# Two units of a gate projection computed with seven block products for eight, in a decoder trunk that TensorE bounds

## The chip, the core and the metric

The kernel runs on one core of a Trainium2 chip. The metric is the device time of one execution in microseconds (us). Of the kernel before there are three runs: 814.84, 815.72 and 815.72, median 815.72 us. Its profiled execution took 816.18 us, of which the profile's span covers 813.3 us; the remaining 2.9 us lie around the span. The engines are called by the profile's names: PE (TensorE), PEld (its weight loads), DVE (VectorE), ACT (ScalarE), POOL (GpSimd) and SP (SyncE, which issues most DMAs).

## The reference

One layer over 256 tokens with model width 2048, all in float32:

```
h = rmsnorm(x);  u = h @ W_in            # conv branch, recurrent branch, two merge gates ga, gb
ya, yb = short conv branch, gated linear recurrence branch
m = sigmoid(ga) * (ya @ W_A) + sigmoid(gb) * (yb @ W_B)
x = x + m @ W_o
gate = sigmoid(rmsnorm(x) @ W_pg)        # "the last gate", 2048 x 2048
x = x + gate * (p @ W_pp)
out = rmsnorm(x)
```

## The kernel before, in words

**Work items.** Every projection is cut into column groups of 512 output columns. A column group is cut into items: one item `c` holds 256 input features, that is two blocks of 128 features by 512 columns, stored side by side in 1024 columns. The program walks a list of items (`items`) in order; `pos` is the place in it. For an item PE multiplies two feature blocks by two token halves (128 tokens each): four block products. A block product is made of three matmuls (`triple`, L1057 to L1061), because each float32 operand is split into a high and a low part: high by high, high by low, low by high. So an item has 12 matmuls of 512 columns. They accumulate in PSUM banks, one bank for each pair of column group and token half.

**Weights.** SP loads weights into tiles called `raw` (128x2048 float32, 1 MB, two items of one column group; pool `wp`, three buffers, L136 and L155). `split` cuts one item: `cut` (L181 to L184) lets ACT copy the block rounded to float32r (`whi`, L182) and lets DVE subtract that from the block (`wlo`, L183). The pair `whi`, `wlo` has four buffers in `wp`; in the last gate six more lie in the pool `late`.

**Lead.** In the loop over `pos`, items up to `pos + ahead(pos)` are split before the matmuls of `pos` are traced. `ahead` (L1053) is three items, and in the last gate it grows by one for every four items, to eight. Loads run four items further. Before the last gate the four buffers hold the lead to three items: a split waits until PE has finished the item before the one it is at.

**Order.** The program is traced in Python; a scheduler then decides each engine's order from the traced order, the dependencies and its own estimates. `step` lets the epilogues (generators, one step for each item) queue behind the last split. `pinned` (L1106) forces ACT and DVE to keep the traced order for the instructions of one loop step; before, it is in force only from the end of the first `ga` group to shortly after the merged products were parked, not in the last gate.

**The stages at the end.** The output projection `W_o` has four column groups O0 to O3 (8 items each). When one is done, `ep_o` adds it to `x` on DVE (L840), squares it and spreads it on ACT (L841, L847), writes it to DRAM in four DMAs and reads it back (`turned`, L317 and L328, both on SP), transposes 32x32 blocks on DVE (L321), and after a lag of three items scales and splits the four feature blocks into the operand `x1T` (`put`, ACT L286 and DVE L287). The last gate, `W_pg`, has four column groups PG0 to PG3 whose stationary operand is `x1T`; item `c` of each needs feature blocks `2c` and `2c+1`. PG0 and PG1 are done one after the other, 8 items each; after each, `ep_pg` takes the sigmoid (ACT L881), multiplies by the parked `p @ W_pp` (DVE L884), adds to `x` (DVE L885), squares (ACT L886) and multiplies by the final gain on POOL (L893). PG3 is walked three times for its halves, and `ep_last`, `last_half` and `last_norm` end the program.

**Seven for eight, as it exists before.** For column groups 1 to 3 of the two merge gates the kernel already treats a column group of `ga` and the same of `gb` as a pair. Over one item place `c` (a "unit") a pair is a 2x2 by 2x2 block product: eight block products. Five of eight units, `SEVEN`, use Winograd's form with seven: four sums of weight blocks and four sums of token blocks are made first (`combine_weights`, L198, helped by adding DMAs; `token_sums`, L748), and the results are combined afterwards (`ep_products`, L719; `ep_gates`, L730). Units with seven are items of kind `S` (7 products, 21 matmuls), units with eight are two items of kind `C` (4 products each).

Of the kernel before, what the change touches and what calls it, by code (L numbers as in the profile page):

```python
# [15 lines left out]
P = 128  # L16
# [7 lines left out]
CW = 512  # L24
# [7 lines left out]
SEVEN = [()] + 3 * [(0, 2, 3, 5, 6)]  # L32
TOGETHER = [(0, 1), (1, 2), (3, 2)]
NARROW, Q = len(LEVELS), 32

# [12 lines left out]
def hybrid_kernel(ctx, tc, xT, x, pT, prm, gfin, masks, w_in, w_a, w_b, w_o, w_pg, w_pp, out):  # L48
# [58 lines left out]
    for gi, (kind, j, w, g, op) in enumerate(groups):  # L107
        if kind == "gb" and SEVEN[j]:
            continue
        for c in range(w.shape[2]):  # L110
            it = {"gi": gi, "kind": kind, "j": j, "c": c, "last": c == w.shape[2] - 1}
            if kind != "ga" or not SEVEN[j]:
                key = ("PP", j // 2) if kind == "PP" else (gi, c // 2)
                items.append(dict(it, w=(w, g, c), raw=key, slot=(j if kind == "PP" else c) % 2))
            elif c in SEVEN[j]:
                items.append(dict(it, kind="S", w=(w, g, c), raw=(gi, c)))
# [10 lines left out]
    def raw_of(pos):  # L127
        it = items[pos]
        if it["raw"] not in loaded:
            if it["kind"] == "S":  # L130
                t = tuple(
                    pools["st"].tile([P, n, CW], F32, tag=tag, bufs=bufs, name=nm(tag))
                    for tag, n, bufs in (("sA", 2, 2), ("sB", 1, 3))
                )
            else:
                t = wp.tile([P, 2, 2 * CW], F32, tag="raw", bufs=3, name=nm("raw"))  # L136
            loaded[it["raw"]] = t
        return loaded[it["raw"]]

    def load(pos):  # L140
        it = items[pos]
        if it["raw"] not in loaded:
            raw, (w, g, c) = raw_of(pos), it["w"]
            if it["kind"] == "S":
                for n, to in enumerate(raw):
                    nc.sync.dma_start(out=to.rearrange("p n x -> p (n x)"), in_=w[g + n, :, c, n * CW :])
            elif it["kind"] == "C":
                for n in range(2):
# [8 lines left out]
    def add_by_dma(behind=None):  # L157
        pos = next((n for n, it in enumerate(items) if it["kind"] == "S" and n not in pair_sums), None)
        if pos is not None:
# [18 lines left out]
    def pair_of(pool, n, tags=("whi", "wlo"), width=2 * CW):  # L178
        return tuple(pool.tile([P, width], F32R, tag=tag, bufs=n, name=nm(tag)) for tag in tags)

    def cut(hi, lo, src):  # L181
        a = nc.scalar.activation(out=hi, in_=src, func=AF.Copy)  # L182
        v = nc.vector.tensor_tensor(out=lo, in0=src, in1=hi.bitcast(F32), op=ALU.subtract)  # L183
        state["splits"] = (a.ins, v.ins)  # L184

    def split(pos, halves=(0, 1)):
        it = items[pos]
        load(pos)
        src = raw_of(pos)
        src = src[0].rearrange("p n x -> p (n x)") if it["kind"] == "S" else src[:, it["slot"], :]  # L190
        if pos not in parts:
            spare = pos >= gate and (pos - gate) % 10 >= 4
            parts[pos] = pair_of(pools["late"], 6) if spare else pair_of(wp, 4)
# [18 lines left out]
    last_group = len(items) - w_pg.shape[2]  # L212
    gate = len(items) - 4 * w_pg.shape[2]
    parked = next(n for n, it in enumerate(items) if it["kind"] == "A" and it["j"] == 3)
# [500 lines left out]

    def quarters(j):
        return [state[n][:, t * CW : (t + 1) * CW] for n in ("ga", "gb") for t in range(NT)]

    def ep_products(j, bk):  # L719
        for n in ("ga", "gb"):  # L720
            state[n] = t4(n, 1)
        a0, a1, b0, b1 = quarters(j)
        nc.scalar.activation(out=a0, in_=bk["P1"], func=AF.Copy)
# [4 lines left out]

    def ep_gates(j, n, bk):
        q = quarters(j)  # L730
        for t in range(NT):
            add(q[2 * n + t], q[2 * n + t], bk["c", n, t])
        for t in range(NT):
            d = q[2 * n + t]
# [10 lines left out]
    def ep_gb(j, psum):  # L745
        return ep_gate(j, "gb", psum)

    def token_sums():  # L748
# [5 lines left out]
        for first, n in TOGETHER:  # L754
# [12 lines left out]
            a11, a12, a21, a22 = Fv[:, :, 0, 0], Fv[:, :, 1, 0], Fv[:, :, 0, 1], Fv[:, :, 1, 1]  # L767
            s1, s2, s3, s4 = (Sv[:, :, i] for i in range(4))
            for out, u, v, op in (
                (s1, a21, a22, ALU.subtract), (s2, s1, a11, ALU.subtract),  # L770
                (s3, a11, a21, ALU.subtract), (s4, a12, s2, ALU.add),
            ):
                nc.vector.tensor_tensor(out=out, in0=u, in1=v, op=op)
            sums_of = tuple(v[:, first : first + n] for v in state["S"])
            fourth = tuple(v[:, 2 * c : 2 * (c + n) : 2, P:] for v in state["hT"])
            for (hi, lo), src in ((sums_of, Sv[:, :, :3]), (fourth, Sv[:, :, 3])):
                nc.scalar.activation(out=hi, in_=src, func=AF.Copy)
# [57 lines left out]
    def ep_o(j, psum):  # L835
# [10 lines left out]
        for t in range(NT):  # L846
            nc.scalar.activation(  # L847
                out=spread(x1, t), in_=blocks(xs[:, t, j * CW : (j + 1) * CW]), func=AF.Copy
            )
        x1 = yield from turned(x1, 3)  # L850
        for c in range(4):
            put(state["x1T"], j * 4 + c, x1[:, c * T : (c + 1) * T], gain(PRM_GPLE, j * 4 + c))
        if j == 3:
            tot = sc(2, "tot2", 1)
# [3 lines left out]
            )  # L858
            state["rstd2"] = rsqrt_of(tot, NT, D, "r2")

    def ep_pp(j, psum):
# [13 lines left out]
    def ep_pg(j, psum):  # L875
        xs, pw, gt = state["x"], state["pw", j], t4()
        junk = t4()
        for t in range(NT):
            s = slice(t * CW, (t + 1) * CW)
            d = xs[:, t, j * CW : (j + 1) * CW]  # L880
            nc.scalar.activation(  # L881
                out=gt[:, s], in_=psum[t], func=AF.Sigmoid, scale=state["rstd2"][:, t : t + 1]
            )
            nc.vector.tensor_tensor(out=gt[:, s], in0=gt[:, s], in1=pw[:, s], op=ALU.mult)  # L884
            nc.vector.tensor_tensor(out=d, in0=d, in1=gt[:, s], op=ALU.add)  # L885
            nc.scalar.activation(  # L886
                out=junk[:, s], in_=d, func=AF.Square,
                scale=D**-0.5, accum_out=state["ss3"][:, t * 6 + j : t * 6 + j + 1],
            )
        yield  # L890
        for t in range(NT):
            d = xs[:, t, j * CW : (j + 1) * CW]
            nc.gpsimd.tensor_tensor(out=d, in0=d, in1=state["gfin"][:, j * CW : (j + 1) * CW], op=ALU.mult)  # L893
# [159 lines left out]
    def ahead(pos):  # L1053

        return LEAD + min(max(pos - gate, 0) // 4, 5)

# [10 lines left out]

    def count_products(j):
        order = [it for it in items if it["kind"] in ("S", "C") and it["j"] == j]
        used.clear()  # L1070
# [15 lines left out]
    def unit_products(pos):  # L1086
        it = items[pos]
        c, h = it["c"], state["hT"]

# [10 lines left out]
        b22, t1, t3, t2, t4_ = sums.pop(pos)  # L1100
        s1, s2, s3 = (tuple(v[:, SEVEN[1].index(c), i] for v in state["S"]) for i in range(3))
        s4 = x_of(0, 1)
        for name, op, part in zip(names, (s4, x_of(0, 0), x_of(1, 0), s1, s3, s2, x_of(1, 1)),
# [15 lines left out]

    active = []  # L1120
    banks = {}
    psums = {}
    done = 0
    for pos, it in enumerate(items[:last_group]):
        mark = len(nc.cur_bb.bb.instructions)
        kind, j, c, last = (it[n] for n in ("kind", "j", "c", "last"))
        _, _, w, g, opname = groups[it["gi"]]
        nch = w.shape[2]
        if pos == gate:
            close_pool("back")  # L1130
            close_pool("m")
            open_pool("late", "left")
        if pos == parked:
# [4 lines left out]
            active.append(unpark())  # L1138
        if pos + 2 < len(items) and items[pos + 2]["kind"] == "S":
# [22 lines left out]
        if pos >= gate and c == 0:  # L1162
            load_pw(j)
        if pos == FIRST + 4:
# [13 lines left out]
        if kind in ("S", "C"):  # L1178
            if c == 0 and it.get("n", 0) == 0:
                count_products(j)  # L1180
                for name, tag in zip(("P6", ("c", 0, 1), "P5", "P7", "P1", ("c", 0, 0), ("c", 1, 0), ("c", 1, 1)), "ggggssss"):
# [36 lines left out]
        if last and kind not in ("S", "C"):  # L1218
# [110 lines left out]
```

## Time and profile before

| what | value |
|---|---|
| median of three runs | 815.72 us |
| profiled execution, its span | 816.18 us, 813.3 us |
| last gate begins on PE | 716.67 us into the span |
| last matmul begins | 804.23 us into the span |
| PE, DVE, ACT, POOL busy in the span | 803.0, 589.0, 458.3, 49.4 us |
| granted PE clock, mean of the span | 0.996 |

Times in the views count from the start of the span. A busy time counts each instruction from its start to its end; matmuls overlap, so the distance between the starts of two of them, and not their duration, is what one of them costs PE. In a timeline row the first number is the start, the second the time to the end of the last instruction of the row, `x4` the number of instructions merged in the row, and the bracket the idle time of the engine before it with what ended it.

### The profile page before, as it was taken

To read this page: it belongs to the slowest core of one execution; us is meant where nothing else is said; L and a number is where in the kernel's file an instruction comes from. 1 tells how busy PE (TensorE), PEld (TensorE's weight loads), DVE (VectorE), ACT (ScalarE), POOL (GpSimd) and SP (SyncE) were. 2 spreads that over 40 slices of the span, in tenths; PEclk is the share of its full clock that TensorE was granted. 3 is DMA by queue.
4 is the path that set the end of the run, shared out by engine and by line. 5 is a ranking of instruction groups with operands and counts; after the bars stand their busy time and mean duration, and the time that the engine had idled before them with its cause. 6 is when DMAs were issued, how large, how long until landed. Compare 5 with 4: busy or idle time off the path is not lost.

```text
span 813.3 us, 10660 instructions
## 1 busy us (share of the span) xinstructions
PE 803.0 (99%) x4059; PEld 664.8 (82%) x4059; DVE 589.0 (72%) x748; ACT 458.3 (56%) x617; POOL 49.4 (6%) x58
## 2 busy tenths in 40 slices
PE   9999999999999999999999999999999999999995
PEld 6888888888888888888888888888888888888885
DVE  6746588767776498767679988987988665677932
ACT  7576476465555466466456456456544456566623
POOL 1000000001000000000021210210000000000310
PEclk9999999999999999999999999999999999999998
DMA  9988565648867555647799996995844779887812
GB/s 337 389 309 290 196 206 168 235 134 274 253 236 255 184 184 201 207 157 262 269 328 295 317 312 209 318 313 203 255 160 173 277 255 323 302 268 255 309 43 103
DMA packets 52659, 198.52 MB, mean 244 GB/s; under 512 B 6784, under 2 KB 16256, under 8 KB 37888
## 3 DMA queue, kind: packets, MB, share of 16 engines
q1 hardware_dynamic: 43200, 174.78, 61.2%
q0 software_dynamic: 6384, 16.25, 8.4%
q10 hardware_dynamic: 3024, 6.82, 2.5%
q8 instruction: 31, 0.51, 0.2%
q14 instruction: 20, 0.16, 0.1%
HBM read 184.19 MB, written 13.63 MB: 243 GB/s over the span
## 4 chain that ended last, share of the span: by engine, by line
PE 96%; issue 1%; DMA 1%; ACT 0%; DVE 0%; POOLq 0%; POOL 0%
PE g L1059 29%; PE g L1061 29%; PE g L1060 29%; PE s L1060 3%; PE s L1061 3%; PE s L1059 3%; DMA raw<-in_w_pp 1%; PE s L497 1%; PE s L598 0%; PE s L617 0%; PE s L616 0%; PE s L615 0%; ACT xs L922 0%; DVE wlo L183 0%; PE s L589 0%
## 5 line engine op out<-in xcount | busy, mean ns | idle before, releaser
L183 DVE TENSOR_TENSOR wlo<-raw,whi 128x1024 fp32r<-128x1024 f32 (+1 forms) x264 | 319.8, 1227 | 160.9 <-ACT whi L182 159.0
L182 ACT ACTIVATE whi<-raw 128x1024 fp32r<-128x1024 f32 (+1 forms) x264 | 272.2, 1049 | 207.4 <-PE g L1061 172.6
L1059 PE MATMUL g<-whi,xh 128*128 128x512 f32 (+1 forms) x738 | 284.0, 385 | 0.0
L1060 PE MATMUL g<-wlo,xh 128*128 128x512 f32 (+1 forms) x738 | 283.9, 385 | 0.0
L1061 PE MATMUL g<-whi,xl 128*128 128x512 f32 (+1 forms) x738 | 283.7, 385 | 0.0
L1061 PEld LDWEIGHTS g<-whi,xl 128*128 128x128 f32 x738 | 138.7, 188 | 27.6
L1059 PEld LDWEIGHTS g<-whi,xh 128*128 128x128 f32 x738 | 138.7, 188 | 27.4
L1060 PEld LDWEIGHTS g<-wlo,xh 128*128 128x128 f32 x738 | 138.7, 188 | 27.3
L1060 PE MATMUL g<-wlo,mh 128*128 128x512 f32 x128 | 49.8, 389 | 0.0
L1061 PE MATMUL g<-whi,ml 128*128 128x512 f32 x128 | 49.8, 390 | 0.0
L1059 PE MATMUL g<-whi,mh 128*128 128x512 f32 x128 | 49.7, 389 | 0.0
L182 ACT ACTIVATE thi<-sA 128x1024 fp32r<-128x1024 f32 x15 | 15.9, 1062 | 32.6 <-DVE sA L714 20.3
L1060 PE MATMUL s<-wlo,xh 128*128 128x512 f32 x84 | 32.7, 389 | 0.0
L1059 PE MATMUL s<-whi,xh 128*128 128x512 f32 x84 | 32.7, 389 | 0.0
L1061 PE MATMUL s<-whi,xl 128*128 128x512 f32 x84 | 32.7, 389 | 0.0
L1061 PEld LDWEIGHTS g<-whi,ml 128*128 128x128 f32 x128 | 23.9, 188 | 5.2 <-DVE ml L791 0.3
L1059 PEld LDWEIGHTS g<-whi,mh 128*128 128x128 f32 x128 | 24.0, 188 | 5.0
L1060 PEld LDWEIGHTS g<-wlo,mh 128*128 128x128 f32 x128 | 24.0, 188 | 5.0
L1060 PE MATMUL g<-wlo,ybTh 128*128 128x512 f32 x64 | 24.9, 390 | 0.0
L1061 PE MATMUL g<-whi,ybTl 128*128 128x512 f32 x64 | 24.9, 390 | 0.0
L1060 PE MATMUL g<-wlo,yaTh 128*128 128x512 f32 x64 | 24.9, 389 | 0.0
L1061 PE MATMUL g<-whi,yaTl 128*128 128x512 f32 x64 | 24.9, 389 | 0.0
(218 smaller groups left out, 906.5 us busy)
## 6 DMA issues: line engine op xcount, KB each, us to landing
raw<-in_w_in SPq DMA_DIRECT2D x66, 1024.0 KB, 5.1
raw<-in_w_o SPq DMA_DIRECT2D x16, 1024.0 KB, 6.1
raw<-in_w_pg SPq DMA_DIRECT2D x16, 1024.0 KB, 6.6
sT<-in_w_in POOLq DMA_DIRECT2D x30, 512.0 KB, 9.6
raw<-in_w_in SPq DMA_DIRECT2D x28, 512.0 KB, 5.8
raw<-in_w_a SPq DMA_DIRECT2D x8, 1024.0 KB, 8.8
raw<-in_w_b SPq DMA_DIRECT2D x8, 1024.0 KB, 8.6
sA<-in_w_in SPq DMA_DIRECT2D x15, 512.0 KB, 7.7
```

The lines of the kernel that those rows point to most:

```text
L182: a = nc.scalar.activation(out=hi, in_=src, func=AF.Copy)
L183: v = nc.vector.tensor_tensor(out=lo, in0=src, in1=hi.bitcast(F32), op=ALU.subtract)
L497: nc.tensor.matmul(out, X[:, 0, h, s], X[:, 1, h, t], start=True, stop=True, tile_position=(0, i * n))
L1059: nc.tensor.matmul(psum, oh, hi, start=first, stop=False)
L1060: nc.tensor.matmul(psum, oh, lo, start=False, stop=False)
L1061: nc.tensor.matmul(psum, ol, hi, start=False, stop=last)
```

## The change

PG0 and PG1 become one pair. Its units `c` = 3 and 5 (`LATE_SEVEN`) are done with seven products, the other six with eight, so the last gate's list has 30 items instead of 32, in the order C C, C C, C C, S(3), C C, S(5), C C, C C, then PG2 and PG3 as before. Every load of the pair brings 512 KB of each column group instead of 1 MB of one. The weight sums are not helped by DMAs: `combine_late` makes them in place in `raw`. For one unit the work is spread over three loop steps: `split` cuts the first column group's block; the next step does two additions, the cut of one block of 512 columns, and two additions; the step after cuts the two blocks of 1024 columns that the sums now fill. `late_sums` makes the token sums for a unit within `ep_o` of O1 (unit 3) and O2 (unit 5). The lag in `ep_o` of O3 becomes seven. `whi`, `wlo` now have four buffers in `wp` and five in `late` and are handed out by `free_pair`; `late` also gets a fourth `raw` buffer. `ahead` grows by at most one until the second S item, and `pinned` is in force from the start of the last gate to that item. `ep_pg` of the first two groups takes four steps instead of two.

```diff
+LATE_SEVEN = (3, 5)
...
-        if kind == "gb" and SEVEN[j]:
+        if kind == "gb" and SEVEN[j] or (kind, j) == ("PG", 1):
             continue
+        units = {"ga": SEVEN[j % len(SEVEN)], "PG": LATE_SEVEN if j == 0 else ()}.get(kind, ())
...
+                n = it["c"] if it["j"] == 0 else 4 + 4 * (it["j"] - 1) + it["c"] // 2
+                spare = it["op"] == "x1T" and n and n % 4 == 0
+                pool, bufs = (pools["late"], 1) if spare else (wp, 3)
+                t = pool.tile([P, 2, 2 * CW], F32, tag="raw", bufs=bufs, name=nm("raw"))
...
+    rings = {"wp": 4 * [-1], "late": 5 * [-1]}
+
+    def free_pair(until):
+        names = [n for n in rings if n == "wp" or n in pools]
+        name = min(names, key=lambda n: rings[n][0])
+        rings[name] = rings[name][1:] + [until if until < last_group else len(items)]
+        return pair_of(pools.get(name, wp), len(rings[name]))
...
+    def combine_late(pos):
+        R = raw_of(pos)
+        (b11, b21), (b12, b22) = ([R[:, n, i * CW : (i + 1) * CW] for i in range(2)] for n in range(2))
+        add(b11, b11, b12)
+        add(b12, b12, b22)
+        ts = [pair_of(pools["late"], 1, ("bhi", "blo"), CW)]
+        cut(*ts[0], b22)
+        add(b22, b11, b22)
+        add(b21, b22, b21)
+        yield
+        for n in range(2):
+            hi, lo = free_pair(pos)
+            cut(hi, lo, R[:, n, :])
+            ts += [(hi[:, i * CW : (i + 1) * CW], lo[:, i * CW : (i + 1) * CW]) for i in range(2)]
+        b22, t1, t4_, t3, t2 = ts
+        sums[pos] = (b22, t1, t3, t2, t4_)
...
-        x1 = yield from turned(x1, 3)
+        x1 = yield from turned(x1, 3 if j < 3 else 7)
         for c in range(4):
             put(state["x1T"], j * 4 + c, x1[:, c * T : (c + 1) * T], gain(PRM_GPLE, j * 4 + c))
+        for c in LATE_SEVEN:
+            if c // 2 == j:
+                yield
+                yield from late_sums(c)
...
+    def late_sums(c):
...
+        add(F.rearrange("p r b t -> p r (b t)"), hi.bitcast(F32), lo.bitcast(F32))
+        yield
+        sums_of(F[:, 0, 0], F[:, 1, 0], F[:, 0, 1], F[:, 1, 1], [Sv[:, i] for i in range(4)])
+        yield
+        cut(*(v[:, LATE_SEVEN.index(c)] for v in state["late sums"]), Sv)
+        yield
...
-        return LEAD + min(max(pos - gate, 0) // 4, 5)
+        return LEAD + min(max(pos - gate, 0) // 4, 5 if pos > settled else 1)
...
+        for q in range(pos + 1, done):
+            if items[q]["kind"] == "S" and items[q]["op"] != "hT" and q not in sums:
+                next(combining.setdefault(q, combine_late(q)), None)
...
-            if kind == "C" and c == nch - 1 and it["n"] == 0:
-                ep_products(j, banks)
+            if pos == settled + 2 or it["op"] == "hT" and kind == "C" and c == nch - 1 and it["n"] == 0:
+                ep_products(it["op"], banks)
             unit_products(pos)
             if kind == "C" and c == nch - 1:
-                ep_gates(j, it["n"], banks)
+                ep_gates(it["op"], it["n"], banks)
...
-        if begun < pos < parked + 8:
+        if begun < pos < parked + 8 or gate <= pos <= settled:
             pinned(mark)
```

More of the change, by code (lines that the diff above doesn't have):

```diff
@@ L157, in add_by_dma @@
     def add_by_dma(behind=None):
-        pos = next((n for n, it in enumerate(items) if it["kind"] == "S" and n not in pair_sums), None)
+        pos = next((n for n, it in enumerate(items) if it["kind"] == "S" and it["op"] == "hT" and n not in pair_sums), None)
         if pos is not None:
@@ L212, in hybrid_kernel @@
     last_group = len(items) - w_pg.shape[2]
-    gate = len(items) - 4 * w_pg.shape[2]
+    gate = next(n for n, it in enumerate(items) if it["op"] == "x1T")
+    settled = max(n for n, it in enumerate(items) if it["kind"] == "S")
     parked = next(n for n, it in enumerate(items) if it["kind"] == "A" and it["j"] == 3)
@@ L746, in ep_gb, with sums_of @@
         return ep_gate(j, "gb", psum)
+    def sums_of(a11, a12, a21, a22, to):
+        s1, s2, s3, s4 = to
+        for out, u, v, op in (
+            (s1, a21, a22, ALU.subtract), (s2, s1, a11, ALU.subtract),
+            (s3, a11, a21, ALU.subtract), (s4, a12, s2, ALU.add),
+        ):
+            nc.vector.tensor_tensor(out=out, in0=u, in1=v, op=op)
     def token_sums():
@@ L767, in token_sums @@
             a11, a12, a21, a22 = Fv[:, :, 0, 0], Fv[:, :, 1, 0], Fv[:, :, 0, 1], Fv[:, :, 1, 1]
[L768 to L774, printed above, removed]
+            sums_of(a11, a12, a21, a22, [Sv[:, :, i] for i in range(4)])
+            three = tuple(v[:, first : first + n] for v in state["S"])
             fourth = tuple(v[:, 2 * c : 2 * (c + n) : 2, P:] for v in state["hT"])
-            for (hi, lo), src in ((sums_of, Sv[:, :, :3]), (fourth, Sv[:, :, 3])):
+            for (hi, lo), src in ((three, Sv[:, :, :3]), (fourth, Sv[:, :, 3])):
                 nc.scalar.activation(out=hi, in_=src, func=AF.Copy)
@@ L1066, in hybrid_kernel, with count_products @@
     used, left = {}, {}
-    def count_products(j):
-        order = [it for it in items if it["kind"] in ("S", "C") and it["j"] == j]
+    def count_products(gi):
+        order = [it for it in items if it["kind"] in ("S", "C") and it["gi"] == gi]
         used.clear()
@@ L1100, in unit_products @@
         b22, t1, t3, t2, t4_ = sums.pop(pos)
-        s1, s2, s3 = (tuple(v[:, SEVEN[1].index(c), i] for v in state["S"]) for i in range(3))
-        s4 = x_of(0, 1)
+        if it["op"] == "hT":
+            s1, s2, s3 = (tuple(v[:, SEVEN[1].index(c), i] for v in state["S"]) for i in range(3))
+            s4 = x_of(0, 1)
+        else:
+            s1, s2, s3, s4 = (tuple(v[:, LATE_SEVEN.index(c), i] for v in state["late sums"]) for i in range(4))
         for name, op, part in zip(names, (s4, x_of(0, 0), x_of(1, 0), s1, s3, s2, x_of(1, 1)),
@@ L1128, in hybrid_kernel @@
         nch = w.shape[2]
+        if kind == "O" and j == 2 and c == 0:
+            close_pool("back")
         if pos == gate:
-            close_pool("back")
             close_pool("m")
```

79 lines of the change are left out of this document (50 added, 29 removed).

## The prediction

> **What bounds the kernel now.** I read the page's busy shares and its chain first, then the table of stretches over the last gate, then PE's timeline.
>
> ```profile
> PE 803.0 (99%) x4059; PEld 664.8 (82%) x4059; DVE 589.0 (72%) x748; ACT 458.3 (56%) x617; POOL 49.4 (6%) x58
> ...
> PE 96%; issue 1%; DMA 1%; ACT 0%; DVE 0%; POOLq 0%; POOL 0%
> ```
> ```profile
> core 0: us, PE busy (x) PEld busy (x) DVE busy (x) ACT busy (x) POOL busy (x), PEclk, DMA share, GB/s
> 700.00:720.00 20.00, 20.00 (x90) 16.57 (x89) 11.12 (x14) 10.70 (x17) 0.00 (x0) 1.00 0.88 302
> 720.00:740.00 20.00, 20.00 (x90) 16.56 (x89) 14.76 (x18) 13.26 (x21) 0.72 (x1) 1.00 0.85 290
> 740.00:760.00 20.00, 20.00 (x90) 16.55 (x89) 15.21 (x14) 11.27 (x16) 4.06 (x2) 1.00 0.71 247
> 760.00:780.00 20.00, 20.00 (x90) 16.57 (x89) 15.61 (x14) 11.47 (x15) 4.29 (x2) 1.00 0.64 228
> 780.00:800.00 20.00, 20.00 (x118) 17.78 (x117) 6.02 (x13) 6.27 (x15) 3.08 (x3) 1.00 0.12 43
> ```
> ```profile
> 716.67 0.39 PE L1059 MATMUL g<-whi,xh 128*128 128x512 f32 x1
> 716.90 0.39 PE L1060 MATMUL g<-wlo,xh 128*128 128x512 f32 x1
> ...
> 792.83 0.28 PE L1059 MATMUL g<-whi,xh 128*128 128x256 f32 x1
> ```
>
> PE makes up 96% of the chain that ended last, and in the last gate it is never idle: 20.00 of 20 us in every stretch, at a granted clock of 1.00. So a matmul that goes is time that goes, and any wait of PE that comes is time that comes. What a matmul costs is the distance of starts. From 716.67 to the first 256-column matmul at 792.83 there are 24 items of 12 and 48 of the last group's first pass, 336 matmuls: 76.16 / 336 = 0.2267 us each. An item of 12 lasts 2.72 us, a unit with seven products (21 matmuls) 4.76.
>
> DVE has 4 to 9 us of each 20 left up to 780. That is little slack for a change that swaps PE work for DVE work in one short stretch, so the prediction is mostly a count of DVE's queue there.
>
> **The change, part by part.** *Removed:* one product for each of two units, 2 x 3 matmuls x 0.2267 = **1.36 us** of PE. Nothing else leaves the chain; this is the most that can be won, 0.17% of the time. What a measurement of this kernel can tell from no change is about 0.2%, 1.63 us, so even the full gain lies inside that.
>
> The Trainium skill, "TensorE: Matmul & The Clock Gate", section "Back-to-back issue gap", gives about 131 ns for each 512-column matmul in a sustained stream of weight loads and matmuls. By that the six would be worth an estimated 0.79 us; the trace's distance of starts differs (0.2267 us), and it decides.
>
> *Added on DVE and ACT.* The prices:
>
> ```profile
> L714 DVE TENSOR_TENSOR sA<-sA x15: 691/691/693, 439.6 to 593.2; 128x512 f32<-128x512 f32 x15
> ...
> L183 DVE TENSOR_TENSOR blo<-sB,bhi x15: 681/683/685, 441.4 to 595.0; 128x512 fp32r<-128x512 f32 x15
> ```
> ```profile
> 413.50 0.28 DVE L773 TENSOR_TENSOR tlo<-thi 128x128 f32<-128x128 f32 x1
> ...
> 414.23 0.28 DVE L773 TENSOR_TENSOR tlo<-thi,tlo 128x128 f32<-128x128 f32 x1
> ```
> ```profile
> 715.25 1.23 DVE L183 TENSOR_TENSOR wlo<-raw,whi 128x1024 fp32r<-128x1024 f32 x1 [1.49 <-ACT whi L182]
> 716.39 1.24 DVE L321 STREAM_TRANSPOSE t<-t 128x1024 f32<-128x1024 f32 x1
> 717.55 1.25 DVE L840 TENSOR_TENSOR xs<-xs,g 128x512 f32<-128x512 f32 x2
> 718.72 1.65 DVE L287 SCALAR_TENSOR_TENSOR xl<-t,prm_t,xh 128x256 fp32r<-128x256 f32 x4
> 720.29 1.22 DVE L183 TENSOR_TENSOR wlo<-raw,whi 128x1024 fp32r<-128x1024 f32 x1
> ...
> 739.05 3.50 DVE L183 TENSOR_TENSOR wlo<-raw,whi 128x1024 fp32r<-128x1024 f32 x3
> ```
> ```profile
> 716.87 1.06 ACT L182 ACTIVATE whi<-raw 128x1024 fp32r<-128x1024 f32 x1 [1.66 <-PE g L1061]
> ...
> 719.44 0.61 ACT L841 ACTIVATE t<-xs 128x512 f32<-128x512 f32 x1
> ...
> 721.62 1.13 ACT L847 ACTIVATE t<-xs 128x512 f32<-128x512 f32 x2
> 722.66 2.94 ACT L182 ACTIVATE whi<-raw 128x1024 fp32r<-128x1024 f32 x3
> ...
> 736.36 0.91 ACT L286 ACTIVATE xh<-t,prm_t 128x256 fp32r<-128x256 f32 x2 [1.50 <-DVE t L321]
> ```
>
> In a queue a 1024-column cut costs DVE (3.50 - 1.23) / 2 = 1.14 us and ACT (2.94 - 1.06) / 2 = 0.94. A 512-column DVE operation costs 0.60 behind an independent one (1.25 - 0.68 = 0.57 in the x2 row at 717.55) and 0.72 behind one whose result it reads (0.69 plus the handover). The four token sums took 1.0 us, 413.50 to 414.51. So one late unit's middle step (four additions, one cut of 512) is 3.3 us, its last step 2 x 1.14 = 2.3, its token sums 0.7 + 1.0 + 0.6 = 2.3. A unit lasts 4.76 us on PE and now needs 1.1 + 3.3 + 2.3 = 6.7 us of DVE, where two items needed 2.3. I count whether the queue is still in time.
>
> Start: the transposition of O2's block at 716.39. It cannot be much earlier, since it waits for the reload issued at 708.46 (below). Then, as in the trace, O3's additions and O2's four puts, to 720.37. Unit 5's token sums need those puts, so they come here: additions and sums to 722.1. The cut of the fourth item (three were cut ahead) follows. In the pinned order its ACT half stands behind O3's squares and spreads: the transposition ends 717.63, then ACT does 4 puts (1.6), 2 squares (1.2), 2 spreads (1.1) and the cut (1.06): 722.6. DVE waits 0.5 for it.
>
> - cuts of items 4, 5, 6 and of the first unit, 4 x 1.14, and the token sums' cut 0.6: 727.8
> - first unit, middle step 3.3: 731.1; cuts of the two items after it 2.3: 733.4; last step 2.3: **735.7**
>
> PE reaches the first unit at 716.67 + 6 x 2.72 = 733.0. The first three of its products need no sums. The fourth needs the first sum block's low part 2.04 + 0.23 later, at 735.3 (there at 734.6), the fifth the second block's at 735.95 (there at 735.7). **In time, by 0.25 us.**
>
> - second unit: first cut 1.1: 736.8; middle step 3.3: 740.1; cut of the next item 1.1: 741.3
> - O3's transposition (two steps are taken at an S item, so its lag of seven ends here) 1.2, the wait for ACT's first put 0.5, four puts 1.6, two small operations of the norm 0.3: 744.9
> - last step: ACT starts after its puts, DVE waits 0.3, then 1.2 and 1.1: **746.4 and 747.5**
>
> PE reaches the second unit at 733.0 + 4.76 + 2 x 2.72 = 743.2. The fourth product wants its block at 745.5 and gets it at 746.4: a wait of 0.9. The fifth then wants 747.1 and gets 747.5: 0.5 more. Together **about 1.5 us of new PE wait**. Behind the unit the lead recovers: each further item costs PE 2.72 and DVE 1.14.
>
> *Loads.* The pair's blocks come as 512 KB DMAs. Their buffer is held longer: the first unit's from its load to 735.7.
>
> ```profile
> raw<-in_w_pg SPq DMA_DIRECT2D x16, 1024.0 KB, 6.6
> ```
> ```profile
> 708.46 0.34 SPq L328 DMA_DIRECT2D t<-turn  x1
> 708.89 13.01 SPq L155 DMA_DIRECT2D raw<-in_w_pg  x3
> 722.78 1.75 SPq L317 DMA_DIRECT2D turn<-t  x4
> 724.99 1.17 SPq L155 DMA_DIRECT2D raw<-in_w_pg  x1
> 729.20 0.34 SPq L328 DMA_DIRECT2D t<-turn  x1
> 729.63 0.38 SPq L155 DMA_DIRECT2D raw<-in_w_pg  x1
> ```
>
> The second unit's block goes into the buffer that the fourth item's cut frees, at about 723.8. SP then issues it at once, as it issued one at 724.99 ahead of O3's reload, and it lands by 731, five us before it is cut. The block that reuses the first unit's buffer is issued at 735.7 and lands at 742.3; its cut comes after 747.5. I cost the loads at nothing; without that cover they are the third rival. Two half loads for one whole add an SP issue of some 0.34 us each (as in the row at 708.46), in a queue that mostly waits.
>
> *The rest, at nothing.* The combination of the seven products (four DVE operations, one ACT copy) and four additions of the ordinary banks are 8 x 0.6 = 4.8 us of DVE, after the second unit; PE then has four to six cut items before it, 11 to 16 us. If that cover were gone they would cost up to 4.8. PSUM: the pair takes eight banks, but those of O2 and O3 are read by 718.8 and first needed at 733.0. `x1T`'s last blocks are put by 744.6 and PE wants them after 749. The token sums of unit 3 fall into the O stage, where DVE idles 1.49 us before each cut (row at 715.25). Nine buffer pairs instead of ten still hold the last group's eight. DVE's 6.02 busy us of the stretch from 780 leave room for a queue that is some 10 us longer.
>
> *Sum:* -1.36 + 1.5 = +0.1. In the profiled execution's own terms 816.18 becomes 816.3; that execution is 0.46 us above the median of the runs, 815.72, so I predict **815.9**.
>
> **The rivals.**
>
> *No new wait (814.4).* The scheduler could take O2's transposition as soon as its reload has landed. The reload is issued at 708.46; O3's, at 729.20, was put to use at 735.08, so 5.9 us bound its landing from above: 714.3. That is 2.1 us before 716.39, and DVE idles 1.49 us there. The whole queue moves up by some 1.5 us and the second unit is in time: 815.72 - 1.36 = 814.4. Against it: DVE took the cut at 715.25 first.
>
> *The second unit's load (817.2).* Its load is traced behind O3's reload, which waits for four DMAs to land (722.78 to 729.20 before, so at about 728 now). If SP keeps that order, the block is issued at 728.5 to 729 and lands 6.6 us later, at 735.5; at up to 8 us for two halves, 737. Its cut, due from 735.7, ends up to 2 us late, and all behind it: +0.5 to +2.5, in the middle 1.5. For it: the queue's order is the scheduler's. Against it: in the trace a load went ahead.
>
> *Slower: DVE waits for ACT at the gate's start (818.2).* The new thing here is that ACT keeps the traced order, so the fourth item's cut, which ACT did at 716.87, stands behind the O3 epilogue, 722.6. I let DVE fill that time with unit 5's token sums. If the scheduler puts them behind the cuts, DVE idles from 720.4 to 722.6 and does the 2.3 us afterwards. The queue is in deficit already, so all of the 2.3 arrives at PE: 3.8 us of wait, +2.4. It decides from 1.5 us of further DVE delay between 716.4 and 745 on.
>
> **How the numbers follow.** Forecast, +0.1 (from -0.6 to +1.1): 0.38. No wait, -1.36: 0.22. Load: 0.20, a little under half of it beyond +1.63. DVE idle: 0.16. Faster for a reason not seen here (below -1.63): 0.04. Slower by over 0.2%: 0.16 + 0.09 = 0.25. Faster by over 0.2%: 0.04. Within: 0.71. The range takes in the first three cases, from 814.2 to 818.1, and leaves out 0.2.
>
> **What would show it.** Matmuls of the last gate: 6 fewer. PE in the stretch from 716 to 760: idle only before the second unit's fourth and fifth products, released by DVE (L183's cut, as numbered then), none before the first unit. DVE without idle time from 717 to 747. The second unit's load issued ahead of O3's reload. If PE waits on `raw` or at the first unit, or for more than 3 us, the forecast is wrong; if its queue shows no wait at all, DVE's count is.

## The result and the profile after

| | before | after |
|---|---|---|
| median of 14 runs each | 815.22 us | 816.87 us |
| lowest, highest | 814.77, 815.99 us | 816.3, 817.66 us |
| profiled execution's span | 813.3 us | 815.3 us |
| last gate begins on PE; last matmul begins | 716.67; 804.23 us | 716.91; 806.27 us |

The ratio is 1.0020, with a 95% interval of 1.0011 to 1.0028: the change makes the kernel slower by 1.65 us, about as little as can be told from nothing. The forecast was +0.1 us, in a range that goes up to 818.1; its 815.9 counts from the 815.72 of the first three runs, which lies 0.5 above the median of all 14.

Lines have moved: the three matmuls of a product are L1122, L1123 and L1124 (L1059 to L1061 before), the cut is L195 on ACT and L196 on DVE (L182, L183), the put L319 and L320 (L286, L287), the transposition L354 (L321), the squares and spreads L880 and L886 (L841, L847). An addition is L747, the token sums proper L790, ACT's copy of the product P1 in `ep_products` L756.

First the page of after: busy time of the engines, and the chain that ended last.

```profile
PE 803.5 (99%) x4053; PEld 663.9 (81%) x4053; DVE 606.2 (74%) x780; ACT 462.8 (57%) x624; POOL 59.5 (7%) x58
...
PE 95%; issue 1%; DVE 1%; ACT 1%; POOLq 0%; POOL 0%; ACTq 0%
```

PE has its six matmuls less (4053 for 4059), and yet DVE and ACT now hold 1% each of the chain: PE waits for them somewhere. Next the table of stretches of after over the last gate: length, then busy time and number of instructions of each engine, the granted clock, the DMA share and GB/s.

```profile
core 0: us, PE busy (x) PEld busy (x) DVE busy (x) ACT busy (x) POOL busy (x), PEclk, DMA share, GB/s
710.00:720.00 10.00, 10.00 (x46) 8.29 (x45) 6.38 (x7) 3.04 (x6) 0.00 (x0) 1.00 0.94 334
720.00:730.00 10.00, 9.41 (x41) 7.14 (x40) 8.39 (x15) 9.53 (x17) 0.00 (x0) 1.00 0.66 217
730.00:740.00 10.00, 10.00 (x46) 8.29 (x45) 9.83 (x12) 4.93 (x6) 0.00 (x0) 1.00 0.97 361
740.00:750.00 10.00, 9.17 (x39) 6.57 (x37) 7.39 (x13) 3.83 (x7) 0.71 (x1) 1.00 0.27 101
750.00:760.00 10.00, 9.79 (x44) 8.03 (x44) 10.00 (x11) 7.01 (x8) 0.00 (x0) 1.00 0.70 253
```

Two places, not one: 720 to 730, and around 750. The clock is 1.00 all along. The busy column shows only 0.59 + 0.83 + 0.21 = 1.63 us of PE's idle time, since a matmul's record outlasts the start of the next. The counts say more: a full stretch has 45 or 46 matmuls, these three have some 5, 7 and 2 fewer, and 14 x 0.2267 is about 3.2 us. PE's timeline at the two places gives the single waits (start, time to the end, line, operands, and the idle time before with its releaser).

```profile
724.85 0.39 PE L1124 MATMUL s<-whi,xl 128*128 128x512 f32 x1
725.29 0.73 PE L1122 MATMUL s<-whi,xh 128*128 128x512 f32 x2
726.55 0.50 PE L1123 MATMUL s<-wlo,xh 128*128 128x512 f32 x1 [0.53 <-DVE wlo L196]
726.89 0.40 PE L1124 MATMUL s<-whi,xl 128*128 128x512 f32 x1
...
746.43 0.39 PE L1124 MATMUL s<-whi,xl 128*128 128x512 f32 x1
747.22 0.50 PE L1122 MATMUL s<-whi,xh 128*128 128x512 f32 x1 [0.40 <-ACT xh L319]
...
748.54 0.40 PE L1124 MATMUL s<-whi,xl 128*128 128x512 f32 x1
749.37 0.51 PE L1122 MATMUL g<-whi,shi 128*128 128x512 f32 x1 [0.43 <-ACT whi L195]
749.71 0.40 PE L1122 MATMUL s<-whi,xh 128*128 128x512 f32 x1
750.32 0.73 PE L1122 MATMUL g<-whi,shi 128*128 128x512 f32 x2 [0.21 <-ACT whi L195]
```

Read the starts, not the brackets. At the fourth item, four distances from 724.85 to 726.89 take 2.04 us where 4 x 0.2267 = 0.91 would do: 1.1 us lost. At the second unit a distance of 0.79 at 747.22, 0.83 at 749.37 and 0.61 at 750.32, with what follows each, lose 0.7, 0.7 and 0.5: 1.9 us. Together 3.03 us, and -1.36 + 3.03 = +1.67, which is the measured +1.65. Over the whole gate the distance from its first matmul to the last went from 87.56 to 89.36 us, +1.80; the 0.13 more lie in many distances that are a few ns longer, which are not counted here.

The rows of ACT of after at these places say what came late.

```profile
719.10 1.71 ACT L319 ACTIVATE xh<-t,prm_t 128x256 fp32r<-128x256 f32 x4 [3.64 <-DVE t L354]
720.71 0.61 ACT L880 ACTIVATE t<-xs 128x512 f32<-128x512 f32 x1
...
723.14 0.63 ACT L195 ACTIVATE shi<-t 128x512 fp32r<-128x512 f32 x1 [0.44 <-DVE t L790]
...
724.20 3.89 ACT L195 ACTIVATE whi<-raw 128x1024 fp32r<-128x1024 f32 x4
...
746.17 0.60 ACT L756 ACTIVATE t<-g 128x512 f32<-128x512 f32 x1 [8.24 <-PE g L1124]
746.67 1.70 ACT L319 ACTIVATE xh<-t,prm_t 128x256 fp32r<-128x256 f32 x4
748.26 3.90 ACT L195 ACTIVATE whi<-raw 128x1024 fp32r<-128x1024 f32 x4
```

And the rows of DVE of after:

```profile
717.83 1.24 DVE L354 STREAM_TRANSPOSE t<-t 128x1024 f32<-128x1024 f32 x1
...
725.27 3.50 DVE L196 TENSOR_TENSOR wlo<-raw,whi 128x1024 fp32r<-128x1024 f32 x3 [0.78 <-ACT whi L195]
...
743.65 1.24 DVE L354 STREAM_TRANSPOSE t<-t 128x1024 f32<-128x1024 f32 x1
747.20 1.69 DVE L320 SCALAR_TENSOR_TENSOR xl<-t,prm_t,xh 128x256 fp32r<-128x256 f32 x4 [2.32 <-ACT xh L319]
```

At the second unit DVE had turned O3's block by 744.89, and ACT could have put it then. But ACT had been standing for 8.24 us before the copy of P1, which reads a product that PE itself had just finished; the puts, and the cuts of the sums behind them, came after it, and DVE stood for 2.32 us. PE waited for ACT, and ACT had waited for PE. At the fourth item ACT's cut began at 724.20. It takes some 1.04 us and so ended at 725.24, 2.6 us after the 722.6 at which the prediction had it done: the transposition was 1.44 us later (717.83 for 716.39), and the token sums' cut, with the wait before it, stood ahead of the weight's and made up the rest.

### The profile page after: what moved, and what is told of

It is laid out like the page before. It is cut to its first block, busy times and chain, and to the rows that moved or that the text cites. A ratio compares the mean times of both kernels' runs of the same rounds, so it can differ in the third digit from the quotient of the medians.

```text
span 815.3 us, 10701 instructions
## 1 busy us (share of the span) xinstructions
PE 803.5 (99%) x4053; PEld 663.9 (81%) x4053; DVE 606.2 (74%) x780; ACT 462.8 (57%) x624; POOL 59.5 (7%) x58
## 4 chain that ended last, share of the span: by engine, by line
PE 95%; issue 1%; DVE 1%; ACT 1%; POOLq 0%; POOL 0%; ACTq 0%
PE g L1122 27%; PE g L1124 27%; PE g L1123 27%; PE s L1123 4%; PE s L1124 4%; PE s L1122 4%; PE s L530 1%; ACT whi L195 0%; PE s L1014 0%; ACT xh L319 0%; DVE wlo L196 0%; PE s L631 0%; PE s L650 0%; PE s L649 0%; PE s L648 0%
## 5 line engine op out<-in xcount | busy, mean ns | idle before, releaser
L196 DVE TENSOR_TENSOR wlo<-raw,whi 128x1024 fp32r<-128x1024 f32 (+1 forms) x266 | 318.4, 1214 | 151.1 <-ACT whi L195 149.3
L195 ACT ACTIVATE whi<-raw 128x1024 fp32r<-128x1024 f32 (+1 forms) x266 | 274.0, 1049 | 201.4 <-PE g L1124 168.3
L1122 PE MATMUL g<-whi,xh 128*128 128x512 f32 (+1 forms) x676 | 260.0, 385 | 0.0
L1124 PE MATMUL g<-whi,xl 128*128 128x512 f32 (+1 forms) x676 | 259.7, 384 | 0.0
L1123 PE MATMUL g<-wlo,xh 128*128 128x512 f32 (+1 forms) x676 | 259.6, 384 | 0.0
L1122 PEld LDWEIGHTS g<-whi,xh 128*128 128x128 f32 x676 | 127.0, 188 | 25.2
L1124 PEld LDWEIGHTS g<-whi,xl 128*128 128x128 f32 x676 | 127.0, 188 | 25.1
L1123 PEld LDWEIGHTS g<-wlo,xh 128*128 128x128 f32 x676 | 127.0, 188 | 24.9
L1123 PE MATMUL s<-wlo,xh 128*128 128x512 f32 x136 | 53.1, 390 | 0.5 <-DVE wlo L196 0.5
L1124 PE MATMUL s<-whi,xl 128*128 128x512 f32 x136 | 53.0, 390 | 0.0
L1122 PE MATMUL s<-whi,xh 128*128 128x512 f32 x136 | 52.5, 391 | 0.5 <-ACT xh L319 0.4
L1123 PE MATMUL g<-wlo,mh 128*128 128x512 f32 x128 | 49.8, 389 | 0.0
L1124 PE MATMUL g<-whi,ml 128*128 128x512 f32 x128 | 49.8, 390 | 0.0
L1122 PE MATMUL g<-whi,mh 128*128 128x512 f32 x128 | 49.5, 389 | 0.0
L195 ACT ACTIVATE thi<-sA 128x1024 fp32r<-128x1024 f32 x15 | 15.9, 1062 | 32.3 <-DVE sA L747 20.1
L1122 PEld LDWEIGHTS s<-whi,xh 128*128 128x128 f32 x136 | 25.5, 188 | 6.4 <-ACT xh L319 0.8
L1123 PEld LDWEIGHTS s<-wlo,xh 128*128 128x128 f32 x136 | 25.5, 188 | 6.3 <-DVE wlo L196 1.0
L1124 PEld LDWEIGHTS s<-whi,xl 128*128 128x128 f32 x136 | 25.5, 188 | 5.5 <-DVE xl L320 0.2
L1124 PEld LDWEIGHTS g<-whi,ml 128*128 128x128 f32 x128 | 24.0, 188 | 5.2 <-DVE ml L830 0.3
L1122 PEld LDWEIGHTS g<-whi,mh 128*128 128x128 f32 x128 | 24.0, 188 | 5.0
L1123 PEld LDWEIGHTS g<-wlo,mh 128*128 128x128 f32 x128 | 24.0, 188 | 5.0
L1124 PE MATMUL g<-whi,ybTl 128*128 128x512 f32 x64 | 24.9, 389 | 0.0
```

Of the source, the lines that this page charges most:

```text
L1122: nc.tensor.matmul(psum, oh, hi, start=first, stop=False)
L1123: nc.tensor.matmul(psum, oh, lo, start=False, stop=False)
L1124: nc.tensor.matmul(psum, ol, hi, start=False, stop=last)
```

## The experiments

Two theories stood after the traces. **The copy**: the second unit's wait comes from an order in ACT's queue, the copy of P1 ahead of O3's puts; the fourth item's from the order that `pinned` forces at the gate's first step. **The queue**: it comes from DVE's amount of new work, as the prediction counted it. Four runs were made on one chip (before: 815.28 us, median of 31), then three on another (before: 815.11 us, median of 27). Each PE wait below is summed as above, from the distances of starts between 700 and 800 us of the run's trace, without those that are only a few ns longer.

**One: no weight sums.** The seven products all read the first column group's cut blocks.

```diff
-        R = raw_of(pos)
...
-        add(b22, b11, b22)
-        add(b21, b22, b21)
+        hi, lo = parts[pos]
+        b11, b21 = ((hi[:, i * CW : (i + 1) * CW], lo[:, i * CW : (i + 1) * CW]) for i in range(2))
         yield
...
-        sums[pos] = (b22, t1, t3, t2, t4_)
+        sums[pos] = (b11, b21, b11, b21, b11)
```

> The change with the weight sums left out: combine_late makes no additions and no cuts, and the unit's seven products all use the two cut blocks of the first column group (so the weight sums are not computed). PE's 21 matmuls, the loads, the banks and the order of items stay. Theory work (PE's new waits come from ACT and DVE, which make the sums and what stands behind them): the waits at the second unit, 1.9 us in the changed kernel, all but vanish; the wait of 1.0 us at the fourth item, ahead of any weight sum, stays. So -1.36 + 1.0, about -0.3 us against before, from -0.6 to +0.3. Rival pair (the pair itself costs: half loads, eight banks, the new order of items): the waits stay, +1.6 us as the changed kernel.

Measured: 815.17 us, ratio 0.9996 (0.9987 to 1.0006). The table of stretches of this run:

```profile
720.00:730.00 10.00, 9.41 (x40) 7.15 (x39) 8.42 (x14) 9.00 (x14) 0.00 (x0) 1.00 0.71 241
...
740.00:750.00 10.00, 10.00 (x46) 8.26 (x44) 8.42 (x13) 8.89 (x13) 0.72 (x1) 1.00 0.93 365
```

The second unit's wait is gone and the fourth item's 1.13 us is there as before. The time lies in the expected range. So the weight sums have no part in the fourth item's wait, and the second unit's wait needs them to be there, whichever theory holds.

**Two: no token sums for the second unit.** Its products read the token sums of the first.

```diff
-            if c // 2 == j:
+            if c // 2 == j and c == LATE_SEVEN[0]:
...
-            s1, s2, s3, s4 = (tuple(v[:, LATE_SEVEN.index(c), i] for v in state["late sums"]) for i in range(4))
+            s1, s2, s3, s4 = (tuple(v[:, 0, i] for v in state["late sums"]) for i in range(4))
```

> The change without the token sums of the second unit: late_sums is made for the first unit alone and the second unit uses the first one's (so the second unit's token sums are not computed). This takes 2.3 us from DVE and one cut from ACT just after the last gate begins. Theory queue (DVE's queue is too long, as predicted): the wait at the fourth item falls from 1.0 to 0.4 and the waits at the second unit from 1.9 to 0.3 or less: -0.7 us against before. Theory copy (the second unit waits because ACT stands still for 8 us behind the copy of the first product, whose time PE sets): only the fourth item's wait falls, by 0.5 to 1.0; the second unit still waits about 1.9, since PE is no faster there: +0.7 to +1.1 us.

Measured: 815.66 us, ratio 1.0006 (0.9996 to 1.0015). ACT's timeline of this run, at the gate's start and around the second unit:

```profile
716.75 0.63 ACT L880 ACTIVATE t<-xs 128x512 f32<-128x512 f32 x1 [1.89 <-DVE xs L879]
...
744.40 0.60 ACT L756 ACTIVATE t<-g 128x512 f32<-128x512 f32 x1 [7.96 <-PE g L1124]
744.90 1.70 ACT L319 ACTIVATE xh<-t,prm_t 128x256 fp32r<-128x256 f32 x4
```

The fourth item's wait is gone, the second unit's is whole, 1.92 us. DVE had 2.3 us less to do by the prediction's prices, ahead of that unit, and it helped nothing there: ACT again stands, for 7.96 us, before the copy. The queue theory fails here. The time, +0.38, lies between the two theories, the copy with +0.7 to +1.1 and the queue with -0.7. The fourth item's wait went whole, so the trace's sum is -1.36 + 1.92 = +0.56, and that lies within the interval of -0.3 to +1.2. At the fourth item more changed than the token sums: O3's squares now run from 716.75, in time that ACT had spent idle, and no longer between the puts and the cut.

**Three: the copy in order.** ACT keeps the traced order for two more steps, and the copy, traced two steps after the second unit, comes after the puts.

```diff
-        if begun < pos < parked + 8 or gate <= pos <= settled:
+        if begun < pos < parked + 8 or gate <= pos <= settled + 2:
```

> The change with the traced order of ACT and DVE kept two loop steps longer, so that ACT's copy of the product P1 stands behind O3's puts, the cuts of the second unit's sums and four further cuts. Theory copy: ACT no longer stands still, O3's puts come 1.8 us earlier, and the waits at the second unit fall from 1.9 to 0.5 or less; the wait of 1.0 at the fourth item stays: +0.1 us against before, from -0.4 to +0.6. Theory queue: DVE has the same work in the same time, so 1.5 us of wait stay at the second unit: +1.1 us.

Measured: 815.43 us, ratio 0.9998 (0.9989 to 1.0008). ACT's timeline and one row of the stretches of this run:

```profile
745.52 1.71 ACT L319 ACTIVATE xh<-t,prm_t 128x256 fp32r<-128x256 f32 x4 [4.80 <-DVE t L354]
747.14 4.84 ACT L195 ACTIVATE whi<-raw 128x1024 fp32r<-128x1024 f32 x5
```
```profile
740.00:750.00 10.00, 10.00 (x45) 8.00 (x44) 9.09 (x15) 5.20 (x9) 0.71 (x1) 1.00 0.39 159
```

The puts now follow the transposition that releases them, the cuts follow the puts, and the second unit's 1.9 us shrink to 0.20. The time is as expected. The work is the same, and from 733 us to the last of these cuts the order of ACT and DVE differs from the change's in the place of the copy alone. The copy's place is the cause of that wait; what is left, 0.2, stands behind DVE's transposition.

**Four: the gate's first step free.** `pinned` begins one step later.

```diff
-        if begun < pos < parked + 8 or gate <= pos <= settled:
+        if begun < pos < parked + 8 or gate < pos <= settled:
```

> The change with the traced order of ACT and DVE not forced in the first loop step of the last gate, so that the scheduler may put the fourth item's cut ahead of O3's squares and spreads, as in the kernel before. If the forced order is what makes the fourth item late, its 1.0 us goes and the second unit's waits stay or shrink a little: +0.3 to +0.8 us against before. If it is the token sums' cut ahead of it on ACT, the wait stays: +1.6 us.

Measured: 815.79 us, ratio 1.0004 (0.9995 to 1.0014). ACT's timeline of this run:

```profile
716.43 1.06 ACT L195 ACTIVATE whi<-raw 128x1024 fp32r<-128x1024 f32 x1 [1.43 <-PE g L1123]
...
721.21 0.61 ACT L880 ACTIVATE t<-xs 128x512 f32<-128x512 f32 x1
...
724.25 0.63 ACT L195 ACTIVATE shi<-t 128x512 fp32r<-128x512 f32 x1 [0.77 <-DVE t L790]
```

Left free, the scheduler puts a cut at 716.43, ahead of O3's squares, as it did before the change; the fourth item's 1.13 us are gone and the second unit's 1.92 stay, as expected. So the forced order made the fourth item late. It did so together with the second unit's token sums: in the second run the order is forced too, without them, and there is no wait either.

**Five: both orders.** Three and four together: `gate < pos <= settled + 2`.

> Both order edits together: the first loop step of the last gate is free, and the traced order is kept two steps longer behind it. The wait at the fourth item (1.0 us) was gone with the first edit alone, and 1.7 of the second unit's 1.9 with the second alone. If the two are independent, as theory copy and the forced order at the gate have it, 0.2 us of wait are left: -1.1 us against before, from -1.4 to -0.6. Theory queue (a DVE queue in deficit passes on whatever is saved ahead of it): earlier items make PE reach the second unit 0.9 us sooner, and the same work is late by that much: 1.1 us of wait, -0.3.

Measured: 813.56 us (813.28 to 814.6, 11 runs), ratio 0.9982 (0.9973 to 0.9990). Its stretches and ACT's timeline:

```profile
720.00:730.00 10.00, 10.00 (x46) 8.29 (x45) 8.87 (x16) 8.50 (x14) 0.00 (x0) 1.00 0.94 313
...
740.00:750.00 10.00, 10.00 (x45) 8.13 (x44) 9.16 (x14) 6.88 (x10) 0.72 (x1) 1.00 0.38 139
```
```profile
743.12 1.71 ACT L319 ACTIVATE xh<-t,prm_t 128x256 fp32r<-128x256 f32 x4 [6.98 <-DVE t L354]
744.74 6.73 ACT L195 ACTIVATE whi<-raw 128x1024 fp32r<-128x1024 f32 x7
```

PE waits for 0.08 us in all, and the kernel is 1.55 us faster than before: the whole gain of six matmuls, 1.36 us, within the interval of -2.2 to -0.8. The median is a little better than the expected range, -1.4 to -0.6, and the wait smaller than the expected 0.2. This version is faster than before, and the changed kernel was slower than before. The gain is 0.18%, just short of the 0.2% that the prediction set as what can be told from no change, though the interval lies wholly below 1.

**Six: more work for DVE.** The version of five, with two additions of 512 columns behind the second unit's token sums, each behind the one before; nothing reads what they leave.

```diff
+        if c == LATE_SEVEN[1]:
+            add(f[:, :CW], f[:, CW:], f[:, :CW])
+            add(f[:, :CW], f[:, CW:], f[:, :CW])
```

> The kernel with both order edits and, right behind the second unit's token sums, two additions of 128x512 on DVE whose result nobody reads, each waiting for the one before: 1.4 us of DVE work ahead of both units. Theory queue (DVE is in deficit there, so each us arrives at PE): 1.4 us more than the kernel with both order edits, +0.3 against before. Rival slack (with ACT flowing and PE's order filling in, DVE has room of a us or more): 0 to 0.5 us more, -1.0 to -0.6.

Measured: 813.98 us, ratio 0.9987 (0.9978 to 0.9996); PE waits 0.48 us, 0.40 more than in five. DVE's timeline of five:

```profile
726.89 1.23 DVE L196 TENSOR_TENSOR wlo<-raw,whi 128x1024 fp32r<-128x1024 f32 x1 [0.95 <-ACT whi L195]
...
741.85 1.24 DVE L354 STREAM_TRANSPOSE t<-t 128x1024 f32<-128x1024 f32 x1
```

and of six:

```profile
724.25 1.42 DVE L747 TENSOR_TENSOR t<-t 128x512 f32<-128x512 f32 x2
...
742.28 1.24 DVE L354 STREAM_TRANSPOSE t<-t 128x1024 f32<-128x1024 f32 x1
```

Of the 1.42 us that were put in, 0.95 went into DVE's own idle time before the cut at 726.89, and O3's transposition came only 0.43 later. Those 0.43 then reached PE almost whole (0.40). So DVE's queue is full behind 727, as the prediction said, and has about 1 us to spare ahead of it, where the prediction had 0.5. The 0.42 us on top of five lie within the slack rival's 0 to 0.5; the -1.13 against before is just below its range, as five itself was.

**Seven: one unit only.** The version of five with `LATE_SEVEN = (3,)`.

```diff
-LATE_SEVEN = (3, 5)
+LATE_SEVEN = (3,)
```

> Both order edits and the first unit alone with seven products (LATE_SEVEN is 3; unit 5 is done with eight): three matmuls fewer than before instead of six, and no weight or token sums of a second unit. By the matmuls -0.68 us, and no theory sees a wait: -0.7, from -1.0 to -0.3.

Measured: 814.44 us, ratio 0.9993 (0.9984 to 1.0002), without any PE wait. That is -0.67 us, as expected; three matmuls are 0.68. The interval still holds 0.

All runs against the sum "matmuls removed plus PE's waits in the trace", in us against before on the same chip:

| version | removed | waits: fourth item, second unit | sum | measured |
|---|---|---|---|---|
| the change | -1.36 | 1.1, 1.9 | +1.67 | +1.65 |
| no weight sums | -1.36 | 1.1, 0 | -0.23 | -0.11 |
| no token sums for the second unit | -1.36 | 0, 1.9 | +0.56 | +0.38 |
| copy in order | -1.36 | 1.1, 0.2 | -0.03 | +0.15 |
| gate's first step free | -1.36 | 0, 1.9 | +0.56 | +0.51 |
| both orders | -1.36 | 0, 0.1 | -1.28 | -1.55 |
| both orders, DVE extra | -1.36 | 0, 0.5 | -0.88 | -1.13 |
| both orders, one unit | -0.68 | 0, 0 | -0.68 | -0.67 |

No row is off by more than 0.27 us, and the intervals reach some 0.7 us to each side. Single verdicts between neighbours of this table therefore rest on the traces; the medians agree with them.

## Why the prediction came out as it did

The form of the sum was right: matmuls gone, minus what PE waits. *The removed term*, 1.36 us, agrees with the versions without waits (-1.55 and, for half of it, -0.67, each with some 0.7 us to either side). Their traces say it more sharply: from the gate's first matmul to the last it is 86.29 us with both orders, 0.08 of it wait, and 86.87 with one unit, where before has 87.56. The estimated 0.79 us by the Trainium skill's "Back-to-back issue gap" ("TensorE: Matmul & The Clock Gate") does not fit these distances, and lies just outside the interval of the -1.55, which is -2.2 to -0.8. *The wait* was forecast at 1.5 us (its parts, 0.9 and 747.5 - 747.1, add to 1.3) and was 3.0; that is the whole miss, and two steps of the prediction failed in it. The time stayed inside the range, but the range is no credit to the mechanism. By the prediction's own signs the forecast was wrong: PE waited already at the fourth item, at the second unit ACT released it and not DVE, and the waits came to a little more than 3 us.

**"The fourth item: 722.6, DVE waits 0.5 for it."** The step had PE in no trouble before the second unit. It counted four puts, two squares and two spreads ahead of the cut on ACT, and left out the token sums' cut, which in the forced order also stands there and itself waits for DVE (0.44 idle before 723.14). It also took the transposition at its old time, 716.39, with O3's additions behind it; it came behind them, at 717.83. The cut ended on DVE at about 726.5 and PE had stood for 1.1 us. The version with the gate's first step free and the one without the second unit's token sums each take this wait away, by different means. This is nearly the rival *Slower: DVE waits for ACT at the gate's start*: its cause, ACT's forced order at the gate's start, was real, but it struck at once, at the fourth item, and not through DVE's queue at the second unit, and it cost 1.1 us and not 2.3. The rival asked whether DVE would be idle, when the first question was whether the item itself would be late.

**"Last step: 746.4 and 747.5 [...] about 1.5 us of new PE wait."** Place and size came out near (1.9 us, behind the second unit's third product), but that was luck: the reason was wrong. The prediction had DVE's queue as the limit, and gave as its sign that DVE is without idle time from 717 to 747; the trace shows DVE idle for 2.32 us before 747.20. What was late was ACT's copy of P1, in a step that the prediction costed at nothing ("The combination of the seven products [...] after the second unit"). It took the copy where the code has it, two steps later. The scheduler took it forward, ahead of O3's puts; ACT then had to wait for PE with O3's puts and the sums' cuts behind it. With the copy in order, the same DVE queue leaves 0.2 us.

That DVE's queue alone costs so little is not because DVE is early. Its count was near: with both orders DVE's two cuts of the second unit's sums end at 747.04 and 748.18 (745.82 + 2.36), where the prediction had 746.4 and 747.5. What differs is PE's order. The rows are of that run, DVE's first:

```profile
745.82 2.36 DVE L196 TENSOR_TENSOR wlo<-raw,whi 128x1024 fp32r<-128x1024 f32 x2 [0.19 <-ACT whi L195]
```
```profile
745.00 0.39 PE L1122 MATMUL s<-whi,xh 128*128 128x512 f32 x1
...
747.36 0.39 PE L1123 MATMUL g<-wlo,shi 128*128 128x512 f32 x1
...
748.50 0.39 PE L1123 MATMUL g<-wlo,shi 128*128 128x512 f32 x1
```

PE does six matmuls of the item behind the unit ahead of the sums' products (745.00 to 746.36), 6 x 0.2267 = 1.36 us of cover, and then the high parts first, so that it reads the low parts at 747.36 and 748.50 only. This order is the scheduler's, and the prediction had the traced one: with it PE would have wanted the first low part at 742.96, where the unit began, + 2.27 = 745.23, and would have waited an estimated 2.3 us for the two. The cover has a price, which the prediction also missed ("PE wants them after 749"): these six read O3's blocks, and in the changed kernel the 0.7 us at 747.22 are a wait for the puts.

The other steps held. The first unit is in time: no wait between 727.4 and 746.4. The *second unit's load* goes ahead of O3's reload, as SP's queue of after shows, so that rival is out; it is issued 2.7 us later than forecast, because the fourth cut was late, and nothing waits for it.

```profile
726.52 1.58 SPq L154 DMA_DIRECT2D raw<-in_w_pg  x2
...
730.54 0.33 SPq L361 DMA_DIRECT2D t<-turn  x1
```

*No new wait* did not occur by itself, and the way that was named for it, an earlier transposition, did not come true; putting the two orders right gives its time (813.56 measured on a chip where before has 815.11).

Left open: why the scheduler placed the copy so early. The trace shows where it stood, not the reckoning that put it there.

## What to carry to other kernels

An instruction that waits at the head of an engine's queue can cost what stands behind it, and not what it does: here a copy of 0.6 us, in a step that was put at nothing, held up ACT, DVE and with them PE, and its place was worth 1.7 us of 815. When costing a step at nothing, ask which instructions follow it in its engine's real order, and what it waits for; where a scheduler makes the order, that includes steps traced later, and a long idle bracket ahead of a short instruction with ready work behind it is the sign. When a region is pinned to the traced order, list everything that stands ahead of the first item needed, for each engine, before counting any amount of work.

## What the runs showed of the hardware

**GpSimd beside a full VectorE.** The final norm's multiplication on POOL, as a group of before and then of after (shortest, median and longest of six, in ns):

```profile
L893 POOL TENSOR_TENSOR xs<-xs,gfin_t x6: 1282/1942/2277, 750.6 to 786.3; 128x512 f32<-128x512 f32 x6
```
```profile
L956 POOL TENSOR_TENSOR xs<-xs,gfin_t x6: 1286/1736/12852, 770.1 to 791.2; 128x512 f32<-128x512 f32 x6
```

The first one of after took 12.85 us, from 770.05 to 782.90 (the profile calls its spans on POOL rough). DVE's timeline of after over this time:

```profile
770.17 1.28 DVE L945 TENSOR_TENSOR t<-t,pw 128x512 f32<-128x512 f32 x2
771.38 1.28 DVE L946 TENSOR_TENSOR xs<-xs,t 128x512 f32<-128x512 f32 x2
772.58 9.17 DVE L196 TENSOR_TENSOR wlo<-raw,whi 128x1024 fp32r<-128x1024 f32 x8
782.57 1.42 DVE L196 TENSOR_TENSOR wlo<-raw,whi 128x1024 fp32r<-128x1024 f32 x1 [0.82 <-ACT whi L195]
```

DVE ran a dozen operations with two inputs from SBUF without a gap and at their usual length, and POOL's ended just after DVE's first pause of 0.82 us. In the version with both orders one took 13.28 us in the same way. The Trainium skill, "SBUF — State Buffer", section "SBUF: two separate sides", says that such DVE operations and GpSimd's share a pair of ports under an exclusive lock, and that the loser blocks for the winner's whole instruction. The rows agree with a blocked loser, though here POOL lost to a whole run of instructions. It is not always POOL that loses: with one unit DVE is as dense from 768.47 on, two of POOL's begin at 768.84 and take 2.0 and 2.28 us, and nine cuts of DVE take 12.61 us where 9 x 1.14 = 10.3 would do. What decides it no run here shows. It cost nothing at the end, since no engine waited for POOL's results; a kernel with GpSimd on its path would have paid an estimated 11 us (12.85 less the median of 1.74).

**After a wait of PE the next distance is longer too.** The matmul that ends a wait is shown with 0.50 us for 0.39, and the one behind it starts 0.33 or 0.34 us later instead of 0.23 (726.55 to 726.89, 747.22 to 747.55, 749.37 to 749.71). So each of the five interruptions costs about 0.11 us on top of its length: some 0.5 of the 3.0 us. Behind such a wait the weight load and its matmul start together (both at 747.22, and again at 749.37), where PEld otherwise runs ahead (its load at 746.20 is for the matmul at 746.43). That may be the reason; no run tests it.
